# Two-layer hybrid decoder on one core: weights as the moving operand, 512 columns a matmul, in branches, projections and feed-forward

## Chip, cores and metric

One NeuronCore of a Trainium2 chip runs the whole program in one launch. The metric is the device time of an execution in microseconds (us); lower is better. Three runs of the kernel before were timed, and one execution was profiled.

## What is computed

The input x has 256 tokens of 1024 features, in float32. Two layers follow, then a last RMSNorm. Of a layer, cut to what matters here (three kinds of attention, a, b and c, stand between):

```python
def _hybrid_layer(x, ...):
    proj = _rms_norm(x, attn_norm) @ w_in          # 1024 -> 6816: q, k, v, latents, gates
    y_a = _diff_attention(...) @ w_branch_a        # 512 -> 1024
    y_b = _dilated_attention(...) @ w_branch_b     # 512 -> 1024
    y_c = _mla(...) @ w_branch_c                   # 512 -> 1024
    g_a, g_b, g_c = split(sigmoid(gates), 3)       # 3 x 1024 columns of proj
    x = x + (g_a * y_a + g_b * y_b + g_c * y_c) @ w_out
    h2 = _rms_norm(x, ffn_norm)
    return x + (silu(h2 @ w_ffn_gate) * (h2 @ w_ffn_up)) @ w_ffn_down    # 2816 hidden
```

## The kernel before

Every product is made in float32 precision from two parts: a weight or an activation is split into a high part `hi` (rounded to the fp32r type) and the rest `lo`, and a product is three fp32r matmuls, hi·hi, hi·lo and lo·hi (`mm3`, L160). A matmul has a stationary operand (128 x 128, loaded into the array) and a moving one that streams through it, 512 columns at most; in the profile `out<-moving,stationary` names them in this order.

**Weights.** `weight_plan` (L51) lists all weights in the order of use, in pieces of 128 partitions x 1024 numbers (512 KB). For each piece SP issues a DMA into one of 5 `raw` buffers, ScalarE (ACT) makes `whi` (`hi_of`, L171), VectorE (DVE) makes `wlo` (`lo_of`, L176), and TensorE (PE) uses both. `take` (L203) hands out the next piece and asks for a later one to be split.

**Activations** are kept with features on the partitions and the 256 tokens along the row (`xT`, four tiles of two feature blocks each). `pair_job` (L211) makes two blocks of 128 output features in one PSUM bank: for each of nk feature blocks, 2 x 3 matmuls, in which a 128 x 128 block of the weight is stationary and 256 tokens move:

```python
for c in range(2):
    s = slice(c * 128, c * 128 + 128)
    self.mm3(ps[:, c * 256:c * 256 + 256], wh[:, s], wl[:, s], xh[k], xl[k], ...)
```

It serves the q and k projections (`qk_proj`), the gates and branches (`branch`, L545), `w_out` and the layer-0 `w_ffn_down` (`out_proj`, L875) and gate and up (`ffn`, L889). The `v_proj` jobs (L463), `mla_up` and the latent inputs do it the other way round: 128 tokens of the activation are stationary and up to 512 weight columns move. So does `tail` (L932), the last layer's `w_ffn_down`.

**Norms.** The normed activation is split before its factor is known: `split_pair` multiplies by the gain alone, and the factor of each token (r) is applied when a result leaves PSUM, by a row `Rb` that is broadcast over the partitions. `norm_sums` (L340) adds squares over the partitions with four tiny matmuls against a tile of ones, `norm_rows` (L360) makes the row `Rb` with two matmuls. At the start GpSimd (POOL) makes the squares of x (L325, L329).

**Order.** The work is written as a stream of pieces (`dense`, `ffn`) from which `pump` takes steps between the stages of attention; a list scheduler then orders the instructions of each engine when the program is built. Near the end `token_major` (L921) transposes the residual on PE, 16 transposes in all, because `tail` produces token-major rows.

Of the kernel before, what the change touches and what calls it, by code (L numbers as in the profile page):

```python
# [34 lines left out]
N_FR = 24  # L35
N_KD = 5
# [14 lines left out]
def weight_plan():  # L51
# [11 lines left out]
    for l in range(DEPTH):  # L63
        block("w_in", l, KT, OFF_C, N_C)
        mixer_in(l, OFF_AQ)
        block("mla_w_uq", l, 3, 0, 768)
        block("mla_w_ukv", l, 2, 0, 1024)
        block("w_in", l, KT, OFF_AV, 512)
        mixer_in(l, OFF_BQ)
        block("w_in", l, KT, OFF_BV, 512)  # L70
        for br, name in BRANCHES:
            for p in range(4):
                block("w_in", l, KT, OFF_G + br * D + p * 256, 256)
                block(name, l, 4, p * 256, 256)
        for p in range(4):
            block("w_out", l, KT, p * 256, 256)
        for p in range(NF // 2):
            block("w_ffn_gate", l, KT, p * 256, 256)
            block("w_ffn_up", l, KT, p * 256, 256)
        if l + 1 < DEPTH:  # L80
            for p in range(4):
                block("w_ffn_down", l, NF, p * 256, 256)
        else:
            block("w_ffn_down", l, NF, 0, 1024)
# [41 lines left out]

def split_rows(t):
    return t.rearrange("p (c t) -> p c t", c=2)


class Build:
    def __init__(self, nc, tc, ctx, x, w, gains, lam, fnorm, cst, out):
        self.nc, self.tc = nc, tc
        self.x_in, self.w_in, self.gains_in = x, w, gains
# [9 lines left out]
        self.fr = ring(N_FR, 512, F32R, "fr")  # L144
        self.kd = ring(N_KD, 1024, F32R, "kd")
# [65 lines left out]
    def pair_job(self, ps, xh, xl, nk):  # L211
        k = 0
        while k < nk:
            for wh, wl in self.take():
                for c in range(2):
                    s = slice(c * 128, c * 128 + 128)
                    self.mm3(ps[:, c * 256:c * 256 + 256], wh[:, s], wl[:, s], xh[k], xl[k],
                             k == 0 and c == 0, k == nk - 1)
                k += 1
# [4 lines left out]
    def setup(self):  # L224
# [3 lines left out]
        self.xT = [cp.tile([128, 2, 256], F32, name=f"xT{p}") for p in range(4)]  # L228
        for p in range(4):
            if p == 0:  # L230
                nc.sync.dma_start(out=self.xT[0][:, 0], in_=self.x_in[:, 0, :])
                self.dma_piece()
                nc.sync.dma_start(out=self.xT[0][:, 1], in_=self.x_in[:, 1, :])
            else:
                nc.sync.dma_start(out=self.xT[p], in_=self.x_in[:, 2 * p:2 * p + 2, :])
# [70 lines left out]
    def split_pair(self, p, src, g0):  # L306
        hi, lo = self.fr.get(), self.fr.get()
        halves = [(slice(c * 256, c * 256 + 256), self.gains[:, g0 + 2 * p + c:g0 + 2 * p + c + 1]) for c in range(2)]
        for c, (cs, g) in enumerate(halves):
            self.hi_of(hi[:, cs], src[:, c], g)  # L310
        for c, (cs, g) in enumerate(halves):
            self.lo_of(lo[:, cs], src[:, c], hi[:, cs], g)
        self.xg += [hi, lo]
        self.xh += [hi[:, 0:256], hi[:, 256:512]]
        self.xl += [lo[:, 0:256], lo[:, 256:512]]

    def fresh_norm(self):
        self.xg, self.xh, self.xl = [], [], []

    def square_pair(self, p, first=False):  # L320
        nc = self.nc
        x = self.xT[p].rearrange("p c t -> p (c t)")
        if first:
            t = self.f.get()
            nc.gpsimd.tensor_tensor(out=t, in0=x, in1=x, op=ALU.mult)  # L325
            if p == 0:
                self.sq = t
            else:
                nc.gpsimd.tensor_tensor(out=self.sq, in0=self.sq, in1=t, op=ALU.add)  # L329
                self.f.put(t)  # L330
            return
        if p == 0:
            self.sq = self.f.get()
            nc.scalar.activation(out=self.sq, in_=x, func=AF.Square)
        else:
            t = self.f.get()
            nc.scalar.activation(out=t, in_=x, func=AF.Square)
            nc.vector.tensor_tensor(out=self.sq, in0=self.sq, in1=t, op=ALU.add)
            self.f.put(t)

    def norm_sums(self):
        nc = self.nc
        ps = self.att.get()
        nc.vector.tensor_tensor(out=self.sq[:, 0:256], in0=self.sq[:, 0:256], in1=self.sq[:, 256:512], op=ALU.add)
        for b in range(2):
            self.mm(ps[:, 2 * b:2 * b + 2], self.sq[:, b * 128:b * 128 + 128], self.ones[:, 0:2], b == 0, True)
        v = self.small()
        nc.vector.tensor_scalar(out=v, in0=ps[:, 0:4:2], scalar1=1.0 / D, scalar2=EPS, op0=ALU.mult, op1=ALU.add)  # L348
        self.att.put(ps)
        self.f.put(self.sq)  # L350
        self.r = self.cp.tile([128, 2], F32, name=f"r{self.n_norm}")
        self.n_norm += 1
        self.rsqrt(self.r, v)
        self.diag = self.fr.get()
# [16 lines left out]
    def first_norm(self, pump):  # L371
        self.fresh_norm()
        for p in range(4):
            self.split_pair(p, self.xT[p], G_ATT)
# [3 lines left out]
            self.square_pair(p, True)  # L378

# [1 line left out]
    def dense(self, l):  # L381
        self.pq = [self.banks.get() for _ in range(2)]
        self.pk = [self.att.get() for _ in range(2)]
        for k in range(KT):
            (wh, wl), = self.take()
            st, sp = k == 0, k == KT - 1
            for b in range(2):
                ts = slice(b * 128, b * 128 + 128)
                h, lo = self.xh[k][:, ts], self.xl[k][:, ts]
# [17 lines left out]
        self.m, self.mh, self.ml = [], [], []  # L407
# [4 lines left out]
    def key_pair(self, src, rows=slice(0, 128)):  # L412
        kd = self.kd.get()
        v = kd[rows].rearrange("p (c f t) -> p c f t", c=2, f=2)
        self.split(v[:, :, 0], v[:, :, 1], src)
# [41 lines left out]
    def v_proj(self, v, paired):  # L457
        pv = [self.banks.get() for _ in range(2)]
        k = 0
        while k < KT:  # L460
            for wh, wl in self.take():
                for b in range(2):
                    ts = slice(b * 128, b * 128 + 128)  # L463
                    self.mm(pv[b], self.xh[k][:, ts], wh, k == 0, False)
                    self.mm(pv[b], self.xh[k][:, ts], wl, False, False)
                    self.mm(pv[b], self.xl[k][:, ts], wh, False, k == KT - 1)
                k += 1
            if k < KT:
                yield
# [75 lines left out]
    def branch(self, o, first, last):  # L545
        nc = self.nc
        for p in range(4):
            bank = self.banks.get()
            yield from self.pair_job(bank, self.xh, self.xl, KT)
            t = self.f.get()  # L550
            nc.vector.tensor_tensor(out=split_rows(t), in0=split_rows(bank), in1=self.Rb, op=ALU.mult)  # L551
            self.banks.put(bank)
            nc.scalar.activation(out=t, in_=t, func=AF.Tanh, scale=0.5)
            yield
            yh = [a[:, c * 256:c * 256 + 256] for a in o[0] for c in range(2)]
            yl = [a[:, c * 256:c * 256 + 256] for a in o[1] for c in range(2)]
            bank = self.banks.get()
            yield from self.pair_job(bank, yh, yl, 4)
            if first:
                self.m.append(self.f.get())  # L560
                nc.vector.scalar_tensor_tensor(out=self.m[p], in0=t, scalar=1.0, in1=bank, op0=ALU.add, op1=ALU.mult)
            else:
                nc.vector.scalar_tensor_tensor(out=t, in0=t, scalar=1.0, in1=bank, op0=ALU.add, op1=ALU.mult)
                nc.vector.tensor_tensor(out=self.m[p], in0=self.m[p], in1=t, op=ALU.add)  # L564
            self.f.put(t)
            self.banks.put(bank)
            if last:
                hi, lo = self.fr.get(), self.fr.get()
                self.split(hi, lo, self.m[p], 0.5)
                self.f.put(self.m[p])  # L570
                self.mh.append(hi)
                self.ml.append(lo)
            yield
        self.fr.put(*o[0], *o[1])
# [146 lines left out]
    def out_tiles(self):  # L721
        return [self.fr.get() for _ in range(2)], [self.fr.get() for _ in range(2)]

    def unit_stages(self, kind, l, h):
# [4 lines left out]
        if kind == "a":  # L729
# [46 lines left out]
            def output():  # L776
# [5 lines left out]
                cs = slice((h % 2) * 256, (h % 2) * 256 + 256)  # L782
                self.split(self.oa[0][h // 2][:, cs], self.oa[1][h // 2][:, cs], pt[:, 0:256], self.gdiff[l])
# [5 lines left out]
        if kind == "b":  # L789
            def scores():  # L790
                k = self.kb[h // 2]
                u["s"] = self.scores(self.half(self.qb, h), k[:, (h % 2) * 512:(h % 2) * 512 + 512], self.tb[h])
                if h % 2 == 1:
                    self.fr.put(*self.qb[h // 2])
                    self.kd.put(k)

            def values():
# [10 lines left out]
                cs = slice((h % 2) * 256, (h % 2) * 256 + 256)  # L808
                self.split(self.ob[0][h // 2][:, cs], self.ob[1][h // 2][:, cs], po[:, 0:256])
# [10 lines left out]
        def scores():  # L820
# [3 lines left out]
            if c == 1:  # L824
                self.fr.put(*q)
                self.kd.put(k)

        def values():
# [16 lines left out]
            if c == 1:  # L845
                cs = slice((p % 2) * 256, (p % 2) * 256 + 256)
                self.split(self.oc[0][p // 2][:, cs], self.oc[1][p // 2][:, cs], t[:, 0:256])
# [228 lines left out]
```

## Time and profile before

| | |
|---|---|
| runs | 917.66, 914.79, 917.59 us; median 917.59 |
| profiled execution | span 916.3 us (the page gives no time beside its span) |
| PE busy | 904.6 us of it (99%), 6954 matmuls |
| DVE, ACT, POOL busy | 648.8 (71%), 503.6 (55%), 76.0 us (8%) |
| read from memory | 152.98 MB |

The span is the time from the first to the last instruction of the profiled execution; it lies 1.3 us under the median of the runs. A matmul's busy time runs from its start to the modelled end of its pipeline, and successive matmuls overlap, so what a matmul costs in a stream is read from start to start, and not from its mean duration.

### The profile page before, as it was taken

The page shows a single profiled execution, that of the slowest core. Times are in us where ns is not written, and L with a number is a line of the kernel's source. Part 1 is how long each engine was busy: PE and PEld are TensorE (multiplying, and loading weights), DVE is VectorE, ACT ScalarE, POOL GpSimd, SP SyncE. Part 2 cuts the span into 40 slices and gives each one's busy share as a digit, 9 for nine tenths or more (in the row PEclk, how much of TensorE's full clock was granted, in tenths as well). Part 3 has the DMA queues.
Part 4 walks back from the last instruction along what each step waited for, and adds up shares of the span by engine and source line. Part 5 has one row for each costly group of instructions (what it writes and reads, how often), then busy time and mean ns, then how long its engine had stood idle before and what let it go on. Part 6 is the DMA issues. An engine that isn't in the chain of part 4 may idle for free.

```text
span 916.3 us, 17319 instructions
## 1 busy us (share of the span) xinstructions
PE 904.6 (99%) x6954; PEld 877.5 (96%) x6954; DVE 648.8 (71%) x1069; ACT 503.6 (55%) x838; POOL 76.0 (8%) x98
## 2 busy tenths in 40 slices
PE   7999999999999999999999999999999999999997
PEld 6988999999999999999999899999999999999886
DVE  7777879866776777755457778896667776677544
ACT  5776768544554444444357867774445544544332
POOL 6730030000000000000011303100000000000000
PEclk8999999999999999999999999999999999999999
DMA  7754443455555555555575454345665665556641
GB/s 236 257 181 142 136 139 116 139 184 185 184 184 176 186 182 182 182 161 188 152 217 164 140 180 133 121 139 155 188 183 168 188 181 182 183 175 205 188 148 46
DMA packets 45440, 155.15 MB, mean 169 GB/s; under 512 B 5168, under 2 KB 6192, under 8 KB 45360
## 3 DMA queue, kind: packets, MB, share of 16 engines
q1 hardware_dynamic: 44928, 153.51, 53.8%
q8 instruction: 54, 0.88, 0.4%
q10 hardware_dynamic: 432, 0.55, 0.2%
q14 instruction: 26, 0.21, 0.1%
HBM read 152.98 MB, written 1.05 MB: 168 GB/s over the span
## 4 chain that ended last, share of the span: by engine, by line
PE 97%; DMA 1%; DVE 0%; issue 0%; ACT 0%; POOLq 0%; SPq 0%; DVEq 0%
PE bank L158 87%; PE att L158 7%; DMA raw<-w 1%; PE att L652 1%; PE att L701 0%; PE att L702 0%; PE att L703 0%; DVE fr L178 0%; PE att L626 0%; PE att L781 0%; PE att L926 0%; DVE wlo L176 0%; ACT whi L171 0%; ACT f L978 0%; POOLq L1071 0%
## 5 line engine op out<-in xcount | busy, mean ns | idle before, releaser
L158 PE MATMUL bank<-fr,whi 128*128 128x256 f32 x3520 | 642.1, 284 | 0.0
L158 PEld LDWEIGHTS bank<-fr,whi 128*128 128x128 f32 x3520 | 549.7, 192 | 0.2
L158 PE MATMUL bank<-fr,wlo 128*128 128x256 f32 x1760 | 499.6, 284 | 0.0
L171 ACT ACTIVATE whi<-raw 128x1024 fp32r<-128x1024 f32 (+3 forms) x296 | 305.9, 1035 | 349.0 <-PE bank L158 225.6
L176 DVE TENSOR_TENSOR wlo<-raw,whi 128x1024 fp32r<-128x1024 f32 (+3 forms) x296 | 355.3, 1203 | 164.5 <-ACT whi L171 163.7
L158 PEld LDWEIGHTS bank<-fr,wlo 128*128 128x128 f32 x1760 | 337.4, 192 | 0.0
L158 PE MATMUL bank<-whi,fr 128*128 128x512 f32 (+2 forms) x368 | 113.9, 377 | 0.4 <-ACT whi L171 0.3
L158 PEld LDWEIGHTS bank<-whi,fr 128*128 128x128 f32 x368 | 69.8, 193 | 10.4 <-ACT whi L171 0.9
L158 PE MATMUL bank<-wlo,fr 128*128 128x512 f32 (+2 forms) x184 | 67.5, 377 | 3.9 <-DVE wlo L176 3.9
L158 PEld LDWEIGHTS bank<-wlo,fr 128*128 128x128 f32 x184 | 35.3, 193 | 9.6 <-DVE wlo L176 5.1
L304 POOL TENSOR_TENSOR r<-small,mhalf 128x2 f32<-128x2 f32 x4 | 3.8, 939 | 488.7 <-DVE small L348 488.7
L171 ACT ACTIVATE fr<-f 64x512 fp32r<-64x512 f32 (+2 forms) x56 | 33.5, 598 | 13.0 <-DVE f L564 4.9
L693 ACT ACTIVATE s<-s,small 128x256 f32<-128x256 f32 x80 | 35.6, 450 | 2.1 <-DVE small L691 1.8
L304 POOL TENSOR_TENSOR small<-small,mhalf 128x2 f32<-128x2 f32 (+1 forms) x12 | 8.2, 684 | 293.0 <-DVE small L967 176.9
L158 PE MATMUL bank<-kd,whi 128*128 128x256 f32 x160 | 29.0, 283 | 0.0
L158 PE MATMUL att<-whi,fr 128*128 128x288 f32 (+1 forms) x88 | 25.7, 304 | 0.0
L176 DVE TENSOR_TENSOR fr<-f,fr 64x512 fp32r<-64x512 f32 (+2 forms) x40 | 25.2, 631 | 0.4
L158 PEld LDWEIGHTS bank<-kd,whi 128*128 128x128 f32 x160 | 25.0, 192 | 0.0
L551 DVE TENSOR_TENSOR f<-bank,row 128x512 f32<-128x512 f32 x24 | 16.5, 688 | 11.4 <-PE bank L158 11.4
L158 PE MATMUL bank<-whi,kd 128*128 128x512 f32 (+1 forms) x80 | 23.9, 364 | 0.0
L905 DVE SCALAR_TENSOR_TENSOR f<-bank,row 128x512 f32<-128x512 f32 x22 | 15.2, 690 | 11.4 <-PE bank L158 11.4
L897 DVE TENSOR_TENSOR f<-bank,row 128x512 f32<-128x512 f32 x22 | 15.2, 691 | 10.6 <-PE bank L158 10.5
(154 smaller groups left out, 825.5 us busy)
## 6 DMA issues: line engine op xcount, KB each, us to landing
raw<-w SPq DMA_DIRECT2D x270, 512.0 KB, 3.6
raw<-w SPq DMA_DIRECT2D x16, 336.0 KB, 3.1
raw<-w SPq DMA_DIRECT2D x6, 384.0 KB, 3.6
raw<-w SPq DMA_DIRECT2D x4, 256.0 KB, 2.6
xT<-x SPq DMA_DIRECT2D x3, 256.0 KB, 6.2
f<-fnorm SPq DMA_DIRECT2D x2, 256.0 KB, 3.6
out<-f ACTq DMA_DIRECT2D x2, 256.0 KB, 2.1
xT<-x SPq DMA_DIRECT2D x2, 128.0 KB, 3.1
```

The lines of the kernel that those rows point to most:

```text
L158: self.nc.tensor.matmul(out, lhsT, rhs, start=start, stop=stop, skip_group_check=True)
L171: self.nc.scalar.activation(out=hi, in_=src, func=AF.Copy, scale=scale)
L176: self.nc.vector.tensor_tensor(out=lo, in0=src, in1=h, op=ALU.subtract)
L304: self.nc.gpsimd.tensor_tensor(out=out, in0=v, in1=self.mhalf[:, 0:v.shape[1]], op=ALU.pow)
L551: nc.vector.tensor_tensor(out=split_rows(t), in0=split_rows(bank), in1=self.Rb, op=ALU.mult)
L652: nc.tensor.transpose(ps[0:96, c, b * 128:b * 128 + 128], src[:, b, 2 * p + c, :], self.ident)
L693: nc.scalar.activation(out=s[:, SL[b]], in_=s[:, SL[b]], func=AF.Exp, bias=mn[:, b:b + 1], scale=-1.0, accum_out=z[:, b:b + 1])
L897: nc.vector.tensor_tensor(out=split_rows(a), in0=split_rows(bank), in1=self.Rb, op=ALU.mult)
L905: nc.vector.scalar_tensor_tensor(out=split_rows(t), in0=split_rows(bank), scalar=0.5, in1=self.Rb, op0=ALU.mult, op1=ALU.mult)
```

## The change

In `branch`, `out_proj` and `ffn` the roles are exchanged. A new `rows_job` keeps 128 tokens of the activation stationary (hi, hi, lo) and moves 512 weight columns, into two banks, one for each half of the tokens. The weight plan has the same bytes in pieces of two feature blocks x 512 columns; gate and up alternate in one array `w_ffn`. `qk_proj` keeps `pair_job`. Results are now token-major, so that the norm's factor is a number per partition (`rh` = r/2 goes into the tanh as its scale, `rr` = r²/2 into the product), and the residual `x_tm` is kept token-major, from a second copy of x that is loaded at the start. What the next product needs feature-major is transposed on PE: the mixed branches (`mixed`), the residual before each norm but the first (`norm_pairs`) and the hidden activations (`hidden_pairs`). Squares are summed along the row by ACT (`squares`). `norm_sums`, `token_major` and POOL's squares go, and `norm_rows` stays for the two attention norms alone. The tiles `fr` and `kd` become one ring of 17 pairs. The core of the diff:

```diff
+    def rows_job(self, ps, x, nk):
+        k = 0
+        while k < nk:
+            for wh, wl in self.take():
+                for b in range(2):
+                    h, lo = (x[k][:, o + b * 128:o + b * 128 + 128] for o in (0, 256))
+                    self.mm(ps[b], h, wh, k == 0, False)
+                    self.mm(ps[b], h, wl, False, False)
+                    self.mm(ps[b], lo, wh, False, k == nk - 1)
+                k += 1
+            if k < nk:
+                yield
...
     def setup(self):
...
         for _ in range(N_RAW - 4):
             self.dma_piece()
+        for b in range(2):
+            nc.sync.dma_start(out=self.x_tm[b], in_=self.xt_in[b])
...
+    def squares(self, n):
+        for b in range(2):
             t = self.f.get()
-            nc.gpsimd.tensor_tensor(out=t, in0=x, in1=x, op=ALU.mult)
...
+            self.nc.scalar.activation(out=t, in_=self.x_tm[b][:, n * 512:n * 512 + 512], func=AF.Square, scale=D ** -0.5,
+                                      accum_out=self.ss[n][:, b:b + 1])
...
+    def transposed(self, src, c0):
+        bank = self.att.get()
+        ps = split_rows(bank)
+        for c in range(2):
+            for b in range(2):
+                self.nc.tensor.transpose(ps[:, c, b * 128:b * 128 + 128], src[b][:, c0 + c * 128:c0 + c * 128 + 128], self.ident)
+        return bank, ps
+
+    def norm_pairs(self, pairs, g0):
+        for p in pairs:
+            bank, ps = self.transposed(self.x_tm, p * 256)
+            self.split_pair(p, ps, g0)
+            self.att.put(bank)
...
     def branch(self, o, first, last):
-        for p in range(4):
-            bank = self.banks.get()
-            yield from self.pair_job(bank, self.xh, self.xl, KT)
-            t = self.f.get()
-            nc.vector.tensor_tensor(out=split_rows(t), in0=split_rows(bank), in1=self.Rb, op=ALU.mult)
...
+        for n in range(2):
+            bank = [self.banks.get() for _ in range(2)]
+            yield from self.rows_job(bank, self.xs, KT)
+            t = [self.f.get() for _ in range(2)]
+            for b in range(2):
+                nc.scalar.activation(out=t[b], in_=bank[b], func=AF.Tanh, scale=self.rh[:, b:b + 1])
...
+            yield from self.rows_job(bank, x, 4)
...
+    def mixed(self, n):
+        for p in range(2):
+            bank, ps = self.transposed(self.m[n], p * 256)
+            t = self.fr.pair()
+            self.split(*fields(t), ps, 0.5)
...
+    def out_proj(self, pairs, nk, g0, late):
...
+        for n in range(2):
+            bank = [self.banks.get() for _ in range(2)]
+            for i, _ in enumerate(self.rows_job(bank, ChunkList(pairs), nk)):
+                if n == 0 and i == 0:
+                    late()
+                if n == 1 and i == 1:
+                    self.norm_pairs((0, 1), g0)
...
+            for b in range(2):
+                x = self.x_tm[b][:, n * 512:n * 512 + 512]
+                self.nc.vector.tensor_tensor(out=x, in0=x, in1=bank[b], op=ALU.add)
...
+    def hidden_pairs(self, a, n):
+        for p in range(n // 256):
+            bank, ps = self.transposed(a, p * 256)
+            self.hp.append(self.fr.pair())
+            self.split(*fields(self.hp[-1]), ps)
...
     def ffn(self):
+        def gated(b, a, g):
+            nc.scalar.activation(out=a, in_=g, func=AF.Tanh, scale=self.rh[:, b:b + 1])
+            nc.vector.scalar_tensor_tensor(out=a, in0=a, scalar=1.0, in1=g, op0=ALU.add, op1=ALU.mult)
+        def product(b, a, u):
+            nc.vector.scalar_tensor_tensor(out=a, in0=a, scalar=self.rr[:, b:b + 1], in1=u, op0=ALU.mult, op1=ALU.mult)
+        for i in range(5):
+            a = [self.f.get() for _ in range(2)]
+            bank = [self.banks.get() for _ in range(2)]
+            for j, _ in enumerate(self.rows_job(bank, self.xs, KT)):
+                yield
+                if j == 1 and self.waiting:
+                    self.hidden_pairs(*self.waiting)
...
-    def token_major(self, b, f):
```

**Where rows moved.** Three places of the instruction lists. First PE inside a job of the feed-forward of layer 0. Before; the moving operand is an activation half (`fr`), the stationary one a 128-column block of a weight piece:

```order
L158 MATMUL bank1_62<-fr13_82,whi3_160 128x256
L158 MATMUL bank1_62<-fr9_78,wlo3_165 128x256
L158 MATMUL bank1_62<-fr15_84,whi4_161 128x256
L158 MATMUL bank1_62<-fr16_85,whi4_161 128x256
L158 MATMUL bank1_62<-fr15_84,wlo4_166 128x256
L158 MATMUL bank1_62<-fr15_84,whi4_161 128x256
L158 MATMUL bank1_62<-fr16_85,whi4_161 128x256
L158 MATMUL bank1_62<-fr15_84,wlo4_166 128x256
```

Now the same engine in the same feed-forward, in a gate job, where the hidden values of the step before (`f4`, `f7`, one for each half of the tokens) are turned over:

```order
L210 MATMUL bank0_61<-whi0_145,fr11_80 128x512
L443 MATMUL att1_66<-ident_188,f4_90 128x128
L443 MATMUL att1_66<-ident_188,f7_93 128x128
L443 MATMUL att1_66<-ident_188,f4_90 128x128
L443 MATMUL att1_66<-ident_188,f7_93 128x128
L443 MATMUL att3_68<-ident_188,f4_90 128x128
L443 MATMUL att3_68<-ident_188,f7_93 128x128
L443 MATMUL att3_68<-ident_188,f4_90 128x128
L443 MATMUL att3_68<-ident_188,f7_93 128x128
L210 MATMUL bank3_64<-whi1_146,fr13_82 128x512
L210 MATMUL bank3_64<-wlo1_151,fr13_82 128x512
L210 MATMUL bank3_64<-whi1_146,fr13_82 128x512
```

Matmuls are half as many and twice as wide, and eight transposes stand together between the second and the third of four pieces of a gate job.

Second, PE at the border from `w_out` to the feed-forward in layer 0, now. `bank2` is the last bank of `w_out`, `x_tm0` and `x_tm1` the residual of the two halves of the tokens, `fr15` the first pair of the normed activation:

```order
L443 MATMUL att3_68<-ident_188,x_tm1_158 128x128
L443 MATMUL att3_68<-ident_188,x_tm0_157 128x128
L443 MATMUL att3_68<-ident_188,x_tm1_158 128x128
L210 MATMUL bank2_63<-whi0_145,fr7_76 128x512
L443 MATMUL att2_67<-ident_188,x_tm0_157 128x128
L443 MATMUL att0_65<-ident_188,x_tm0_157 128x128
L210 MATMUL bank3_64<-whi1_146,fr15_84 128x512
L210 MATMUL bank3_64<-wlo1_151,fr15_84 128x512
L210 MATMUL bank0_61<-whi1_146,fr15_84 128x512
L210 MATMUL bank0_61<-wlo1_151,fr15_84 128x512
L443 MATMUL att2_67<-ident_188,x_tm1_158 128x128
```

All 16 transposes of this norm stand within 22 rows around the end of `w_out`, the first feed-forward matmuls among them; before, the four pairs were split as each pair of `w_out` was finished, without a transpose.

Third, ACT at the start, now, where the five first weight pieces are split and the sixth follows (`raw0` for the second time):

```order
L223 ACTIVATE whi3_148<-raw3_143 128x672
L223 ACTIVATE whi4_149<-raw4_144 128x672
L392 ACTIVATE f4_90,small1_107<-x_tm0_157 128x512
L392 ACTIVATE f6_92,small2_108<-x_tm0_157 128x512
L392 ACTIVATE f5_91,small1_107<-x_tm1_158 128x512
L392 ACTIVATE f7_93,small2_108<-x_tm1_158 128x512
L223 ACTIVATE whi0_145<-raw0_140 128x672
```

Before, the sixth piece was split right after the fifth; the four squares, which need the second copy of x, now stand ahead of it.

## Rows read from the trace of the kernel before

**Rows 1.** The page: span, PE's share, and the chain that ended last, by engine

```profile
span 916.3 us, 17319 instructions
...
PE 904.6 (99%) x6954; PEld 877.5 (96%) x6954; DVE 648.8 (71%) x1069; ACT 503.6 (55%) x838; POOL 76.0 (8%) x98
...
PE 97%; DMA 1%; DVE 0%; issue 0%; ACT 0%; POOLq 0%; SPq 0%; DVEq 0%
```

**Rows 2.** What PE waited for, whole span: total us, times, longest us

```profile
PE bank L158 <- DVE wlo L176: 3.9, 4, 2.1
PE bank L158 <- DVE ones L240: 1.0, 1, 1.0
PE bank L158 <- ACT whi L171: 0.3, 1, 0.3
```

**Rows 3.** The largest group of matmuls by form, PE: count, busy us, mean ns

```profile
L158 PE MATMUL bank<-fr,whi 128*128 128x256 f32 x3520 | 642.1, 284 | 0.0
```

**Rows 4.** The chain in order of time, layer 1's feed-forward: start us, us, what

```profile
743.41 0.44 PE att L926 x4
743.85 17.28 PE bank L158 x144
```

**Rows 5.** Timeline of PE in `v_proj` of layer 0, 512 columns: start us, us

```profile
76.91 0.39 PE L158 MATMUL bank<-wlo,fr 128*128 128x512 f32 x1
...
78.27 0.39 PE L158 MATMUL bank<-wlo,fr 128*128 128x512 f32 x1
```

**Rows 6.** Timeline of PE in `tail`, 512 columns

```profile
904.62 0.61 PE L158 MATMUL bank<-whi,fr 128*128 128x512 f32 x2
...
906.66 0.39 PE L158 MATMUL bank<-whi,fr 128*128 128x512 f32 x1
```

**Rows 7.** One tile's view, PE reads of xT: duration ns min/median/max

```profile
L926 PE MATMUL att<-ident,xT x16: 271/272/273, 743.2 to 796.7; 128*128 128x128 f32 x16
```

**Rows 8.** Timeline of PE around `norm_sums` of layer 0's feed-forward

```profile
280.25 0.51 PE L158 MATMUL att<-ones,f 128*128 128x2 f32 x4
...
280.82 0.40 PE L158 MATMUL bank<-fr,whi 128*128 128x256 f32 x2
```

**Rows 9.** By stretch: its us, busy us of PE, PEld, DVE, ACT, POOL; PEclk, DMA, GB/s

```profile
0.00:15.00 15.00, 10.63 (x53) 9.34 (x54) 10.16 (x14) 9.39 (x17) 8.17 (x11) 1.00 0.80 258
15.00:22.00 7.00, 6.00 (x22) 5.57 (x22) 6.88 (x8) 1.64 (x3) 5.32 (x6) 0.52 0.61 185
22.00:29.00 7.00, 7.00 (x48) 7.00 (x48) 3.61 (x13) 3.65 (x6) 4.94 (x5) 0.99 0.94 350
96.00:178.50 82.50, 82.50 (x666) 80.54 (x665) 73.08 (x194) 60.29 (x148) 10.28 (x12) 1.00 0.40 129
...
280.30:407.00 126.70, 126.70 (x1058) 126.70 (x1058) 89.33 (x105) 58.85 (x67) 0.71 (x1) 1.00 0.57 182
```

**Rows 10.** Timeline of PE at the start, weight pieces of the latent inputs

```profile
14.11 0.44 PE L158 MATMUL bank<-wlo,fr 128*128 128x384 f32 x1 [2.12 <-DVE wlo L176]
...
17.93 0.69 PE L158 MATMUL bank<-wlo,fr 128*128 128x384 f32 x1 [1.00 <-DVE wlo L176]
...
28.94 0.40 PE L158 MATMUL bank<-fr,whi 128*128 128x256 f32 x2
```

**Rows 11.** Timeline of DVE at the start

```profile
9.86 2.58 DVE L178 SCALAR_TENSOR_TENSOR fr<-xT,gains,fr 128x256 fp32r<-128x256 f32 x2
...
13.98 2.93 DVE L178 SCALAR_TENSOR_TENSOR fr<-xT,gains,fr 128x256 fp32r<-128x256 f32 x2
```

**Rows 12.** Timeline of ACT at the start: the sixth weight piece

```profile
13.64 0.76 ACT L171 ACTIVATE whi<-raw 128x672 fp32r<-128x672 f32 x1 [0.34 <-DMA raw<-w]
```

**Rows 13.** Groups by form, DVE: count, busy us, mean ns

```profile
L551 DVE TENSOR_TENSOR f<-bank,row 128x512 f32<-128x512 f32 x24 | 16.5, 688 | 11.4 <-PE bank L158 11.4
...
L178 DVE SCALAR_TENSOR_TENSOR fr<-att,gains,fr 128x256 fp32r<-128x256 f32 x10 | 4.4, 475 | 0.0
```

**Rows 14.** Groups by form, ACT

```profile
L337 ACT ACTIVATE f<-xT 128x512 f32<-128x512 f32 x9 | 5.5, 616 | 0.0
```

More of the change, by code (lines that the diff above doesn't have):

```diff
@@ L71, in weight_plan @@
         for br, name in BRANCHES:
-            for p in range(4):
[L73 to L79, printed above, removed]
+            for n in range(2):
+                block("w_in", l, KT, OFF_G + br * D + n * 512, 512)
+                block(name, l, 4, n * 512, 512)
+        for n in range(2):
+            block("w_out", l, KT, n * 512, 512)
+        for n in range(2 * FF // 512):
+            block("w_ffn", l, KT, n * 512, 512)
         if l + 1 < DEPTH:
-            for p in range(4):
-                block("w_ffn_down", l, NF, p * 256, 256)
+            for n in range(2):
+                block("w_ffn_down", l, NF, n * 512, 512)
         else:
@@ L124, in put, with __init__, get, pair @@
         self.free_tiles.extend(tiles)
+class PairRing:
+    def __init__(self, tiles):
+        self.whole = list(tiles)
+        self.halves = [(t[:, 0:512], t[:, 512:1024]) for t in tiles]
+        self.free = deque((i, h) for i in range(len(tiles)) for h in range(2))
+    def get(self):
+        free = set(self.free)
+        for lone in (True, False):
+            for i, h in self.free:
+                if not lone or (i, 1 - h) not in free:
+                    self.free.remove((i, h))
+                    return self.halves[i][h]
+        raise IndexError("no half is free")
+    def pair(self):
+        free = set(self.free)
+        for i, h in self.free:
+            if (i, 1 - h) in free:
+                self.free.remove((i, h))
+                self.free.remove((i, 1 - h))
+                return self.whole[i]
+        raise IndexError("no pair is free")
+    def put(self, *aps):
+        for a in aps:
+            for i, t in enumerate(self.whole):
+                if a is t:
+                    self.free.extend([(i, 0), (i, 1)])
+                for h in range(2):
+                    if a is self.halves[i][h]:
+                        self.free.append((i, h))
+def chunks(pairs):
+    return [t[:, c * 512:c * 512 + 512] for t in pairs for c in range(2)]
+class ChunkList:
+    def __init__(self, pairs):
+        self.pairs = pairs
+    def __getitem__(self, k):
+        return self.pairs[k // 2][:, (k % 2) * 512:(k % 2) * 512 + 512]
+def fields(t):
+    v = t.rearrange("p (c f t) -> p c f t", c=2, f=2)
+    return v[:, :, 0], v[:, :, 1]
 def split_rows(t):
@@ L341, in norm_sums @@
[L341 to L346, printed above, removed]
+        t = self.fr.pair()
+        hi, lo = fields(t)
+        gains = [self.gains[:, g0 + 2 * p + c:g0 + 2 * p + c + 1] for c in range(2)]
+        for c, g in enumerate(gains):
+            self.hi_of(hi[:, c], src[:, c], g)
@@ L436, in qk_proj @@
             bank = self.banks.get()
-            yield from self.pair_job(bank, self.xh, self.xl, KT)
+            yield from self.pair_job(bank, self.xs, KT)
             ps = split_rows(bank)
@@ L458, in v_proj @@
         pv = [self.banks.get() for _ in range(2)]
[L459 to L469, printed above, removed]
+        yield from self.rows_job(pv, self.xs, KT)
         for b in range(2):
@@ new lines, in ffn @@
+        a = [self.f.get() for _ in range(2)]
+        bank = [self.banks.get() for _ in range(2)]
+        for j, _ in enumerate(self.rows_job(bank, self.xs, KT)):
+            yield
+            if j == 1:
+                self.hidden_pairs(*self.waiting)
+        self.fr.put(*self.xg)
+        for b in range(2):
+            gated(b, a[b][:, 0:256], bank[b][:, 0:256])
+            product(b, a[b][:, 0:256], bank[b][:, 256:512])
+        self.banks.put(*bank)
+        self.waiting = (a, 256)
+        yield
@@ L933, in tail @@
+    def tail(self):
         nc = self.nc
@@ L1059 @@
     a = {k: np.asarray(v) for k, v in inputs.items()}
+    gate, up = a["w_ffn_gate"], a["w_ffn_up"]
+    a["w_ffn"] = np.concatenate([m[:, :, c:c + 512] for c in range(0, FF, 512) for m in (gate, up)], axis=2)
     w = pack_weights(a)
```

255 lines of the change are left out of this document (101 added, 154 removed).

## The prediction, made before the change was run

> **What bounds the kernel now.** I read the page first, and in it PE's share and the chain that ended last [rows 1]. PE is busy for 904.6 of 916.3 us, and 97% of the chain is PE. That alone doesn't prove that PE is the limit, since busy times of pipelined matmuls overlap. So I read what PE waited for next [rows 2]: the waits come to 5.2 us in the whole span, and they lie at the start. Between the start and the end the time is the number of matmuls times the distance from one start to the next; whoever wants it shorter has to change one of the two.
>
> That distance is what the change is about. The largest group by form [rows 3] says 284 ns for a matmul of 256 columns, but that is the duration, of which more than half overlaps with the next. In the chain 144 such matmuls take 17.28 us [rows 4]: **0.1200 us each**. For 512 columns the trace has the very form that the change spreads, activation still and weights moving: six starts in `v_proj` from 76.91 to 78.27 are 1.36 us [rows 5], and nine in `tail` from 904.62 to 906.66 are 2.04 us [rows 6]. Both give **0.2267 us**. At the full 2.4 GHz, 256 columns stream in 0.1067 us and 512 in 0.2133, so each matmul pays a fixed 13.3 ns whatever its width, and two matmuls of 256 joined in one save it once: 0.2400 - 0.2267 = 0.0133 us.
>
> Last I read who would be late if PE were faster [rows 9]. In the feed-forward stretch from 280.3 us DVE is busy for 89.3 of 126.7 us, ACT for 58.9, and the DMA engines for 57%. In attention, from 96 us, DVE is the nearest, 73.1 of 82.5 us.
>
> **The change, part by part.**
>
> *Matmuls.* `pair_job` issues 6 matmuls for each feature block and 256 output columns. The jobs that change have, in a layer, 12 x 48 + 12 x 24 = 864 in the branches, 4 x 48 = 192 in `w_out` and 22 x 48 = 1056 in gate and up; `w_ffn_down` of layer 0 has 4 x 132 = 528. That is 2 x 2112 + 528 = 4752 matmuls of 256 columns, which become 2376 of 512. The instruction lists agree (438 matmuls of 512 columns before, 2814 now). All of it is on the path: 2376 x 0.0133 = **-31.6 us**.
>
> *Transposes added.* 16 in each of the two `mixed` steps' layers (32), 16 for each of three norms (48), 44 for the hidden values of each layer (88): 168. In the stream four transposes take 0.44 us [rows 4]. 168 / 4 x 0.44 = **+18.5 us**, on PE and so on the path too.
>
> *PE work removed.* The 16 transposes of `token_major`, 4 x 0.44 = 1.8 us. `norm_sums`, four times: from 280.25 to 280.82 us stand its tiny matmuls and one of 256 columns [rows 8], so 0.57 - 0.12 = 0.45 us each, 1.8 us. `norm_rows` before the two feed-forwards, 4 x 0.12 = 0.5 us. Together **-4.1 us**.
>
> *Evictions and splits.* DVE no longer multiplies by `Rb`: for 512 gate and up columns it did ten passes of 512 numbers at 0.69 us [rows 13] and now does six, four from the banks and two for the splits of the transposed values. ACT has four squares at 0.62 us [rows 14] for each norm, as it had for all but the first, which POOL did. This is hidden work, cost nothing: PE's wait rows don't name it [rows 2]. Weight bytes are the same, and are to arrive 0.1200 x 2 / 0.2267 = 1.06 times as fast; 182 GB/s in the feed-forward stretch becomes 193, and the start has reached 258 and 350 [rows 9]. Cost nothing as well; if DVE's cover went in attention (73.1 of 82.5 us), what PE saves there, some 10 jobs' pieces, would be lost, under 2 us.
>
> *The new waits.* Every transposed value goes bank, DVE, PE, ACT and DVE, PE. In the rows of the feed-forward two of four pieces of a gate job lie before the transposes, 24 matmuls or 5.4 us, against two DVE passes of 0.69: covered, nothing. The narrow places are the three borders from `w_out` or `w_ffn_down` to what follows. There the last addition into `x_tm` (0.69 us) has only three wide matmuls and some transposes before the transposes that need it, and the first feed-forward matmul follows its split at a similar distance. Bounds: 0 where it just fits, and the addition and the first split in full where it doesn't, 0.69 + 0.48 [rows 13] = 1.2 us. I take 0.5 each, since the list shows nearly enough work ahead: **+1.5 us**.
>
> *The start.* Two things pull apart. POOL's squares go, and beside them DVE was slow: two splits of 256 took 2.58 and 2.93 us [rows 11], where one takes 0.475 undisturbed [rows 13]. That is 1.6 and 2.0 us too long on a chain for which PE waited 2.12 and 1.00 us [rows 10]; and from 15 to 22 us, after these waits, PE's granted clock was 0.52, its lower level of 1.2 GHz [rows 9], which costs about half of 7 us. On the other side the second copy of x, 1.05 MB, is queued ahead of the sixth weight piece, and ACT's four squares, which wait for it, stand ahead of that piece's split, which already waited for its DMA before [rows 12]. At 258 GB/s that is 4.1 us. Bounds: a gain of 3.1 for the two waits and 3.4 for the clock, were the weights in time; a loss of 4.1 for the bytes and another 3.4 for a second stretch at the low clock. In between PE has slack, as the latent inputs end at 28.94 us [rows 10] and their 96 matmuls, half of 384 columns and half of 288, need 48 x (0.160 + 0.120 + 2 x 0.0133) = 14.7 us at full clock. I take **-1.0 us**, near the middle, since each wait that goes is met by one that comes.
>
> *Sum:* -31.6 + 18.5 - 4.1 + 1.5 - 1.0 = -16.7 us. On the span, 916.3 becomes 899.6. The median of the runs is 1.3 above the profiled span, so the forecast is **900.9 us**.
>
> **The rivals.**
>
> *Transposes cost their duration (slower).* A transpose here loads a new stationary block for only 128 columns. Its duration is 272 ns [rows 7], its distance in the stream 0.11 us [rows 4], because four stand together and overlap. If the new ones, which read tiles just written and are in places strewn singly between wide matmuls, don't overlap, 152 more of them cost 152 x (0.272 - 0.11) = 24.6 us more: 925.5 us. It decides from 0.22 us per transpose on, where the saving of 16.7 is used up. Against it: the rows of four, and single ones in the list have a wide matmul of 0.2267 us beside them, under which a load can run. The Trainium skill ("TensorE: Matmul & The Clock Gate", Part 4: PE-mode transpose) gives about 275 ns for a transpose inside a kernel. By that rule the change would lose 152 x 0.165 = 25 us against my sum and be slower than before; the trace agrees with the figure as a duration, and denies it as a price. Chance 3%.
>
> *The fixed cost isn't per matmul.* If the 13.3 ns were not saved by joining, the matmuls would give nothing and the transposes remain: 916.3 + 18.5 - 4.1 + 1.5 - 1.0 + 1.3 = 932.5 us. Two places of the trace with 512 columns deny it, to a nanosecond [rows 5, 6]. The same page (Back-to-back issue gap) puts a fixed cost of about 2.5 ns on a matmul: by that the joining would be worth 5.9 us, and the change would be slower, 926.6 us; the measured 13.3 decides. Chance 1%.
>
> *Waits at every crossing.* There are 22 places where PE turns values over: ten in each layer, and two more for the norm of layer 1. If each exposed one DVE pass of 0.69 us, 15.2 us would go: 916.1, no change. For it: DVE also splits a weight piece of 1.2 us in between, which may stand in front. Against it: the 5.4 us of cover at 10 of the 22. Chance 4%.
>
> *Starved start.* Both losses at the start in full: 900.9 + 1.0 + 7.5 = 909.4 us. For it: the sixth piece already waited on its DMA [rows 12]. Chance 10%.
>
> *Fluent start.* Both gains: 900.9 + 1.0 - 6.5 = 895.4 us. Against it: the extra bytes. Chance 10%.
>
> **How the numbers follow.** The forecast has the remaining 72%. Its own spread is the borders (0 to 3.6 us), the transposes (0.10 to 0.12 us each, 1.7 us either way) and the start. The range reaches to the fluent start with cheap borders and transposes, 895.4 - 2 = **893**, and to the starved one, **909**. Left out are the first three rivals and the two ends' tails. Faster by over 0.3% of the median, which is about what a measurement of this kernel can tell from none, is below 914.8: forecast, both starts and part of the crossings, 0.93. Within it: the rest of the crossings, 0.03. Slower: 0.04.
>
> **What would show it.** Right: half as many matmuls of 512 columns in the branches, `w_out` and feed-forward, at 0.2267 us from start to start; four transposes in 0.44 us; a feed-forward stretch without PE waits; DVE's share down. Wrong: waits of PE for DVE or ACT after 30 us; a granted clock below 1.0 beyond the start; the first q and k matmul well after 28.9 us (starved) or before 26 (fluent); transposes that delay the next matmul by over 0.22 us each.

## The result, and the profile after

| | before | after |
|---|---|---|
| median of the runs | 917.62 us (914.79 to 918.12, 4 runs) | 895.41 us (894.39 to 896.65, 4 runs) |
| span of the profiled execution | 916.3 us | 894.8 us |

The ratio is 0.9775, with a 95% interval of 0.9752 to 0.9798: the change makes the kernel 2.2% faster, against 1.8% forecast. 895.41 us lies in the range of 893 to 909, 5.5 us below the forecast of 900.9.

Page of the changed kernel, to be held against [rows 1]: span, busy time by engine, chain that ended last.

```profile
span 894.8 us, 12732 instructions
...
PE 886.5 (99%) x4710; PEld 763.9 (85%) x4710; DVE 591.9 (66%) x990; ACT 504.5 (56%) x852; POOL 66.4 (7%) x91
...
PE 97%; DMA 1%; issue 1%; SPq 0%; ACT 0%; DVE 0%; POOLq 0%; POOL 0%
```

PE is the bound as before, with 97% of the chain. It has 2244 matmuls fewer, and they are wider, as the groups by form show (count, busy us, mean ns; against [rows 3]):

```profile
L210 PE MATMUL bank<-whi,fr 128*128 128x512 f32 x1876 | 592.4, 393 | 0.0
L210 PE MATMUL bank<-wlo,fr 128*128 128x512 f32 x938 | 366.4, 392 | 0.0
...
L443 PE MATMUL att<-ident,f 128*128 128x128 f32 x120 | 16.2, 272 | 0.0
...
L443 PE MATMUL att<-ident,x_tm 128*128 128x128 f32 x48 | 6.9, 272 | 0.0
```

1876 + 938 are the 2814 matmuls of 512 columns, 120 + 48 the 168 transposes. What they cost is read in the chain (start us, us, what), here in the feed-forward of layer 0, against [rows 4]:

```profile
290.49 0.87 PE att L443 x8
291.36 21.80 PE bank L210 x96
313.16 0.87 PE att L443 x8
```

Eight transposes take 0.87 us, 0.109 each, and 96 wide matmuls 21.80 us, 0.2271 each. No other engine stands between them. What PE waited for in the whole span (total us, times, longest), against [rows 2]:

```profile
PE bank L210 <- ACT whi L223: 1.1, 2, 0.9
PE bank L210 <- DVE ones L309: 1.0, 1, 1.0
```

These 2.1 us were 5.2, and none lies after 17 us: neither the borders nor the other crossings cost a wait. The stretches, against [rows 9] (columns as there):

```profile
0.00:15.00 15.00, 12.99 (x72) 12.07 (x73) 8.15 (x17) 10.45 (x20) 0.29 (x5) 1.00 0.86 303
15.00:22.00 7.00, 6.84 (x44) 6.29 (x43) 5.37 (x14) 5.44 (x10) 1.82 (x2) 1.00 1.05 399
22.00:29.00 7.00, 7.00 (x59) 7.00 (x58) 5.32 (x14) 6.84 (x18) 6.72 (x7) 1.00 0.88 332
...
280.30:407.00 126.70, 126.70 (x582) 105.24 (x582) 75.44 (x78) 58.42 (x66) 0.00 (x0) 1.00 0.63 191
```

In the feed-forward PE is busy without a gap, DVE has gone from 89.3 to 75.4 us of 126.7, and weights come at 191 GB/s, where 193 was worked out. The start is where the surprise lies: PE's clock stays at 1.00, POOL is nearly idle until 15 us, and the DMA engines bring 399 GB/s where they brought 185.

One sign that the prediction counts as wrong did come, a granted clock below 1.0 beyond the start: it is 0.66 from 55 to 60 us, with PE busy throughout. The kernel before has such a fall too, 0.80 and 0.86 from 60 to 65 and 65 to 70 us, so it is no difference between the two.

PE at the start, from the timeline; the last row is the first q and k matmul, as in [rows 10]:

```profile
8.52 0.44 PE L210 MATMUL bank<-whi,fr 128*128 128x384 f32 x1 [0.94 <-ACT whi L223]
...
16.57 0.44 PE L210 MATMUL bank<-whi,fr 128*128 128x384 f32 x1 [0.15 <-ACT whi L223]
...
22.72 0.40 PE L210 MATMUL bank<-fr,whi 128*128 128x256 f32 x2
```

And DVE's timeline, against [rows 11]:

```profile
9.27 0.88 DVE L230 SCALAR_TENSOR_TENSOR fr<-f,gains,fr 128x256 fp32r<-128x256 f32 x2
...
10.83 0.88 DVE L230 SCALAR_TENSOR_TENSOR fr<-f,gains,fr 128x256 fp32r<-128x256 f32 x2
```

Two splits take 0.88 us, where they took 2.58 and 2.93.

**Where the time went.** The first q and k matmul is the mark that divides the span: PE's work ahead of it is the same in both kernels, up to the norm's sums. It moved from 28.94 to 22.72 us, so 6.2 of the 21.5 us were won ahead of it and 15.3 behind it.

### The profile page after: what moved, and what is told of

It reads as the page before. It is cut to its first block, busy times and chain, and to the rows that moved or that the text cites. A ratio compares the mean times of both kernels' runs of the same rounds, so it can differ in the third digit from the quotient of the medians.

```text
span 894.8 us, 12732 instructions
## 1 busy us (share of the span) xinstructions
PE 886.5 (99%) x4710; PEld 763.9 (85%) x4710; DVE 591.9 (66%) x990; ACT 504.5 (56%) x852; POOL 66.4 (7%) x91
## 3 DMA queue, kind: packets, MB, share of 16 engines
HBM read 154.03 MB, written 1.05 MB: 173 GB/s over the span
## 4 chain that ended last, share of the span: by engine, by line
PE 97%; DMA 1%; issue 1%; SPq 0%; ACT 0%; DVE 0%; POOLq 0%; POOL 0%
PE bank L210 85%; PE att L210 7%; PE att L443 2%; DMA x_tm<-xt 1%; PE att L718 1%; PE att L767 0%; PE att L769 0%; PE att L768 0%; ACT f L392 0%; SPq L242 0%; PE att L692 0%; PE att L851 0%; DVE x_tm L1043 0%; SPq L302 0%; ACT x_tm L1058 0%
## 5 line engine op out<-in xcount | busy, mean ns | idle before, releaser
L210 PE MATMUL bank<-whi,fr 128*128 128x512 f32 (+1 forms) x2032 | 632.6, 387 | 1.1 <-ACT whi L223 1.1
L228 DVE TENSOR_TENSOR wlo<-raw,whi 128x1024 fp32r<-128x1024 f32 (+2 forms) x294 | 353.3, 1203 | 250.3 <-ACT whi L223 249.1
L223 ACT ACTIVATE whi<-raw 128x1024 fp32r<-128x1024 f32 (+2 forms) x294 | 305.0, 1040 | 309.8 <-PE bank L210 255.3
L210 PEld LDWEIGHTS bank<-whi,fr 128*128 128x128 f32 x2032 | 380.4, 188 | 73.9 <-ACT whi L223 1.6
L210 PE MATMUL bank<-wlo,fr 128*128 128x512 f32 (+1 forms) x1016 | 390.6, 386 | 0.0
L210 PEld LDWEIGHTS bank<-wlo,fr 128*128 128x128 f32 x1016 | 191.3, 188 | 36.3 <-DVE wlo L228 0.9
L210 PE MATMUL bank<-fr,whi 128*128 128x256 f32 x512 | 95.3, 285 | 0.0
L210 PEld LDWEIGHTS bank<-fr,whi 128*128 128x128 f32 x512 | 80.1, 191 | 0.2
L210 PE MATMUL bank<-fr,wlo 128*128 128x256 f32 x256 | 73.0, 285 | 0.0
L210 PEld LDWEIGHTS bank<-fr,wlo 128*128 128x128 f32 x256 | 49.0, 191 | 0.0
L614 ACT ACTIVATE f<-bank,rh 128x512 f32<-128x512 f32 x24 | 16.3, 689 | 8.7 <-PE bank L210 8.5
```

The costliest lines, as they stand in the source:

```text
L210: self.nc.tensor.matmul(out, lhsT, rhs, start=start, stop=stop, skip_group_check=True)
L223: self.nc.scalar.activation(out=hi, in_=src, func=AF.Copy, scale=scale)
L228: self.nc.vector.tensor_tensor(out=lo, in0=src, in1=h, op=ALU.subtract)
L614: nc.scalar.activation(out=t[b], in_=bank[b], func=AF.Tanh, scale=self.rh[:, b:b + 1])
```

## The experiments

The theory is the sum of the prediction with the fluent start in place of its own. The rivals are that another amount per matmul was won and another lost per transpose, so that two errors hide each other; and that the start owes its gain to something else than POOL. Beside the experiments the kernel before ran again, with medians of 915.25, 916.11 and 916.44 us (13, 19 and 13 runs).

**e1_halves: the wide matmuls cut in two.** All else, transposes and layouts too, stays as in the changed kernel.

```diff
-                    self.mm(ps[b], h, wh, k == 0, False)
-                    self.mm(ps[b], h, wl, False, False)
-                    self.mm(ps[b], lo, wh, False, k == nk - 1)
+                    w = 256 if halves else 512
+                    for c in range(512 // w):
+                        s = slice(c * w, c * w + w)
+                        self.mm(ps[b][:, s], h, wh[:, s], k == 0 and c == 0, False)
+                        self.mm(ps[b][:, s], h, wl[:, s], False, False)
+                        self.mm(ps[b][:, s], lo, wh[:, s], False, k == nk - 1)
```

> The changed kernel with each 512-column matmul of the exchanged jobs issued as two of 256 columns, activation still held, weights still moving; v_proj keeps 512. Same products and order, 2376 matmuls more. If the gain of the joining is a fixed 13.3 ns per matmul: +31.6 us, 895.4 becomes about 927, so slower than the kernel before by some 1%. If the gain came from elsewhere (the evictions without the broadcast row, the order, the start): within 3 us of 895.

Measured: 927.27 us (926.9 to 927.38, 4 runs), 31.9 us above the changed kernel, and 1.0116 of the kernel before (1.0099 to 1.0133). The chain of its feed-forward:

```profile
299.09 0.87 PE att L446 x8
299.97 23.03 PE bank L210 x192
```

192 matmuls of 256 columns in 23.03 us are 0.1199 each; the same columns in 96 matmuls took 21.80. So the joining is worth about what the sum said, and without it the change would be a loss: the transposes would be paid for nothing.

**e2_twice: every new transpose issued twice**, into the same place.

```diff
-            for b in range(2):
+            for b in (0, 0, 1, 1):
```

> The changed kernel with each of the 168 added transposes issued twice into the same place. If a transpose costs its distance in a stream, 0.11 us, as four in 0.44 us: +18.5 us, about 914. If it costs its duration, 0.272 us: +45.7 us, about 941. If transposes run in holes of the stream: no change, 895.

Measured: 914.31 us (912.72 to 914.83, 10 runs), 18.9 us above the changed kernel for 168 more transposes: 0.1125 us each. Its chain:

```profile
291.78 1.75 PE att L443 x16
293.52 21.81 PE bank L210 x96
```

16 stand in 1.75 us, 0.109 each, and the wide matmuls behind them are not slower; 168 x 0.109 = 18.3 us. The price per transpose is the distance in the stream and not the duration.

**e3_pool_squares: POOL's squares put back** into the changed kernel's start. Their result is not used; only the work is there.

```diff
+            t = self.f.get()
+            self.nc.gpsimd.tensor_tensor(out=t, in0=self.x0[p], in1=self.x0[p], op=ALU.mult)
+            if p == 0:
+                sq = t
+            else:
+                self.nc.gpsimd.tensor_tensor(out=sq, in0=sq, in1=t, op=ALU.add)
+                self.f.put(t)
+        self.f.put(sq)
```

> The changed kernel with POOL's four squares and three sums of x at the start put back, their result unused. If their load on POOL made DVE slow at the start and so cost PE waits and the low clock: the first q and k matmul comes 3 to 7 us later than 22.7 us, the granted clock falls below 1.0 between 10 and 25 us, and the time rises to 898 to 902. If the start became shorter for another reason (the token-major norm, the order of the rows): 895, first q and k matmul at 22.7.

Measured: 899.74 us (898.78 to 900.57, 4 runs), 4.3 us above the changed kernel. DVE's timeline shows the splits of [rows 11] slow again:

```profile
10.60 2.70 DVE L230 SCALAR_TENSOR_TENSOR fr<-f,gains,fr 128x256 fp32r<-128x256 f32 x2
...
15.05 1.91 DVE L230 SCALAR_TENSOR_TENSOR fr<-f,gains,fr 128x256 fp32r<-128x256 f32 x2
```

PE's timeline shows the same wait for a weight's low part back, and the mark at 26.72 us, 4.0 later:

```profile
15.19 0.45 PE L210 MATMUL bank<-wlo,fr 128*128 128x384 f32 x1 [2.35 <-DVE wlo L228]
...
26.72 0.40 PE L210 MATMUL bank<-fr,whi 128*128 128x256 f32 x2
```

PE's waits for DVE's low parts come to 3.7 us, where it had none. ACT's squares waited twice for a buffer that POOL held, 0.5 us each, which is a side effect of this experiment. The clock did not fall: in the profiled execution it stayed at 1.00 from 10 to 25 us, against that part of the expectation, so a low clock at the start is no part of the 4.3 us. The profiled span is 897.2 us, only 2.4 above the changed kernel's, because this execution lacks the fall of the clock behind the start (897.2 - 26.72 = 870.5 us behind the mark, against 872.1).

**e5_before_act_squares: the same from the other side**, in the kernel before. The squares of x are made by ACT and added by DVE.

```diff
-            self.square_pair(p, True)
+            self.square_pair(p)
```

> The kernel before with one part of the change alone: the squares of x at the start are made by ACT and added by DVE, not by POOL; the rest as before. If POOL's squares slowed DVE and so the start: the first q and k matmul comes 3 to 6 us before 28.9 us and the time falls to 912 to 915 (ratio about 0.995). If they did not: 917.6, or slower by the 2 us of additions that DVE now has at the start.

Measured: 913.5 us (912.39 to 915.55, 10 runs), 0.9977 of the kernel before (0.9965 to 0.9988), 2.6 us. Part of the 2.6 can be the clock: 6 of those 19 runs of the kernel before, and none of these 10, had a mean granted clock under 0.994. Two splits take 0.87 us, although DVE has the additions on top, PE waits for no low part, and the mark lies at 23.35 us (28.94 in [rows 10], 27.10 in e7 below). Not all of that reaches the end, as PE's timeline shows behind the mark:

```profile
23.35 0.40 PE L158 MATMUL bank<-fr,whi 128*128 128x256 f32 x2
...
26.92 0.33 PE L626 MATMUL att<-ident,f 128*128 128x128 f32 x1 [0.55 <-ACT f L585]
...
29.27 0.39 PE L158 MATMUL att<-fr,ones_r 128*128 128x256 f32 x1 [0.58 <-DVE fr L178]
```

Two waits, 1.1 us together, come next, which the changed kernel doesn't have.

**e4_xt_late: the second copy of x behind the sixth weight piece**, its squares behind that piece's split.

```diff
-        for b in range(2):
-            nc.sync.dma_start(out=self.x_tm[b], in_=self.xt_in[b])
...
+            if p == 2:
+                for b in range(2):
+                    self.nc.sync.dma_start(out=self.x_tm[b], in_=self.xt_in[b])
```

> The changed kernel with the second copy of x loaded after the sixth weight piece and ACT's four squares behind that piece's split. If the 1.05 MB and the squares ahead of the sixth piece still cost PE time: 0.5 to 4 us faster than 895.4. If the start has slack for them: 895, or a little slower, as the norm's factor comes later.

Measured: 895.56 us (894.01 to 895.74, 4 runs) against 895.41: the medians show no difference. The profiled executions do: the mark comes 0.9 us earlier, at 21.84, and the span is 893.8, 1.0 less. ACT's timeline has the split of the sixth weight piece at 12.47 us:

```profile
12.47 0.77 ACT L223 ACTIVATE whi<-raw 128x672 fp32r<-128x672 f32 x1 [0.31 <-DMA raw<-w]
```

The changed kernel has it at 15.77, two pieces in a row:

```profile
15.77 1.47 ACT L223 ACTIVATE whi<-raw 128x672 fp32r<-128x672 f32 x2
```

So the copy and its squares do make that piece 3.3 us later. But PE, with the five pieces before it to work through, gets to it only at about 16.3 us and waits 0.15. The chain of the changed kernel runs through the copy at this place:

```profile
5.54 7.63 DMA x_tm<-xt
```

PE thus has slack for most of the delay, and not for all of it: the copy costs about 0.9 us by one profiled execution of each kernel, which the medians of four runs each don't confirm.

**e6_before_more_bytes: the bytes alone**, as a load of 1.05 MB into four free buffers in the kernel before, behind the fifth weight piece. Nothing reads it.

```diff
+        dead = [self.f.get() for _ in range(4)]
+        for i, t in enumerate(dead):
+            nc.sync.dma_start(out=t, in_=self.xt_in[i // 2][:, (i % 2) * 512:(i % 2) * 512 + 512])
+        self.f.put(*dead)
```

> The kernel before with 1.05 MB more loaded at the start behind the fifth weight piece, where the change loads its second copy of x; nobody reads it. If the DMA queue is full there, as the forecast assumed with 258 GB/s: +2 to +4 us, 920 to 922. If it has room: 917.6, the sixth weight piece landing less than 1 us later than at 13.6 us.

Measured: 916.52 us (914.94 to 918.93, 10 runs), 1.0007 of the kernel before (0.9994 to 1.002): the time shows no cost. The other part of the expectation failed. The sixth weight piece was to land less than 1 us later, and ACT gets to split it at 16.32 us, 2.7 us later than in [rows 12]:

```profile
16.32 2.46 ACT L171 ACTIVATE whi<-raw 128x672 fp32r<-128x672 f32 x3 [3.00 <-DMA raw<-w]
```

Its stretches:

```profile
0.00:15.00 15.00, 11.46 (x55) 10.18 (x56) 10.06 (x14) 8.71 (x15) 7.95 (x12) 1.00 0.88 291
15.00:22.00 7.00, 5.33 (x35) 4.77 (x33) 4.34 (x7) 2.94 (x4) 1.94 (x2) 1.00 0.80 272
```

291 and 272 GB/s stand where the kernel before had 258 and 185: over these 22 us the DMA engines had room for the bytes, although the piece behind them came later. The delay hardly reaches PE, which waits for DVE here: the mark lies at 27.42 us. PE's clock is 1.00 from 15 to 22 us, although POOL works and PE waits 3.7 us for DVE. That made the 0.52 of [rows 9] doubtful as a property of the kernel, and so both kernels were profiled once more.

**e7_before_again and e8_after_again: both kernels unchanged.**

> The kernel before once more, to see which part of its start is the same in a second execution. If the low granted clock (0.52 from 15 to 22 us) belongs to the kernel, the clock is low again and the first q/k matmul starts at 28.9 us. If it belonged to that one execution, the clock is 1.00 throughout, the first q/k matmul starts at 27 to 27.5 us as in the run with more bytes, and the span is about 914.5 us. The waits for the weights' low parts stay in both cases (3 to 4 us in total). The time equals the kernel before.

> The changed kernel once more. The start is expected to repeat if POOL's work was what slowed it: first q/k matmul at 22 to 23 us, granted clock 1.00, waits of PE of 2 us in total, span 894 to 896 us. If the first profile was a lucky one, the mark lies at 24 us or later.

Measured: 915.06 us (914.36 to 916.22, 10 runs), 0.9985 of the kernel before's other runs (0.9973 to 0.9997), and 895.76 us (894.71 to 896.79, 4 runs). The start of the kernel before in this second execution, stretches:

```profile
0.00:15.00 15.00, 10.79 (x53) 9.67 (x54) 10.42 (x14) 9.51 (x17) 8.33 (x11) 1.00 0.80 258
15.00:22.00 7.00, 5.29 (x35) 5.01 (x34) 6.92 (x8) 1.55 (x3) 5.35 (x6) 1.00 0.59 176
```

and PE's timeline:

```profile
14.14 0.44 PE L158 MATMUL bank<-wlo,fr 128*128 128x384 f32 x1 [2.12 <-DVE wlo L176]
...
17.96 0.44 PE L158 MATMUL bank<-wlo,fr 128*128 128x384 f32 x1 [1.71 <-DVE wlo L176]
...
27.10 0.40 PE L158 MATMUL bank<-fr,whi 128*128 128x256 f32 x2
```

The waits are there again, the second 0.7 us longer, and PE's waits for low parts come to 4.9 us, more than the 3 to 4 expected; the low clock is not. The mark comes 1.8 us earlier (0.3 earlier than in e6), and the span is 914.4. The changed kernel has its mark at 22.92 us and a span of 895.0. So the waits belong to the kernel and the low clock to the execution. From e7 to the changed kernel the mark moves by 4.4 us and the rest by 15.2 (914.4 - 27.10 = 887.3 against 894.8 - 22.72 = 872.1). Each of these two executions has one fall of the clock behind the mark, to 0.66 in a stretch of 5 us (60 to 65 and 55 to 60 us), so the 15.2 compares like with like.

## Why the prediction was right, and where a term was off

The direction and the range were right. The median lies 5.5 us below the forecast: 4.8 of them come from the start (-6.2 us, where -1.0 and the 0.45 of the first `norm_sums` stood), 0.7 from the distance of median and span (0.6 after, 1.3 assumed), and nothing from the rest (-15.3, where -15.2 stood). The 0.7 is no property of the kernels: each run that is listed with its span is 1.7 to 1.9 us longer than it, so the distance only tells where the profiled execution lies among the runs.

What came is the rival of the fluent start, to which the prediction gave 10%, with its sign, the mark before 26 us. That its 895.4 us were met so closely is luck: of its two gains the waits gave more than the 3.1 us set, the clock gave less than its 3.4, and what the clock gave belongs to one execution.

- **Joining the matmuls, -31.6 us: right.** e1 takes it back and costs 31.9 us by the medians and 925.4 - 894.8 = 30.6 by the profiled spans. The profile has 0.1199 and 0.2271 us a matmul. The fixed cost per matmul is 2 x 0.1199 - 0.2271 = 12.7 ns by these rows, and 31.9 / 2376 = 13.4 ns by the runs. The Trainium skill ("TensorE: Matmul & The Clock Gate", Back-to-back issue gap) has about 2.5 ns, for the gap of a single matmul and not for a stream with weight loads; by it e1 would have cost an estimated 2376 x 2.5 ns = 5.9 us. For this kernel's fp32r matmuls the measurement decides. The rival that joining saves nothing falls.
- **Transposes, +18.5 us: right.** e2 gives 18.9 us for as many. The rival that they cost their duration would have had e2 at 168 x 0.272 = 46 us. The 275 ns of the Trainium skill (same page, Part 4: PE-mode transpose) agree with the 272 ns of a row's duration and are not what one costs between others.
- **PE work removed, borders and crossings, -4.1 + 1.5 + 0 us: right in sum.** The borders show no wait, so the +1.5 was not spent there. That the rest of the span comes out as forecast all the same needs 1.5 us from elsewhere, and where is not shown. Up to 1.0 may be the joining, by the 30.6 above and by the feed-forward's 0.2271 us a matmul for 0.2267; but 89 wide matmuls without a transpose among them, from 269.70 to 289.87 us, start 0.2266 us apart.
- **Evictions, splits, weight traffic, 0: right.** DVE's share fell, and PE waits for nobody in the feed-forward.
- **The start, -1.0 us: the term that was mis-sized. It measured -6.2, the 0.45 of the first `norm_sums` included.** The two gains were named rightly: the waits, and the clock. The failed step is the balance, "each wait that goes is met by one that comes". The wait that was to come is PE's for the sixth weight piece, behind the second copy of x, and the 4.1 us for it were wrong twice. First, a later piece is not a waiting PE: the piece is 3.3 us later through the copy and its squares (e4), and PE waits 0.15 us for it and is about 0.9 later in all by the profile of e4. The slack of PE, which the prediction itself names, covers the rest. Second, 258 GB/s was taken as the ceiling of the DMA engines. It is the mean over a stretch that begins with 2 us at 16 GB/s and in which the queue waits 1.5 us for a free weight buffer. A narrow stretch of the kernel before, 10 to 12 us, shows 402:

```profile
10.00:12.00 2.00, 1.99 (x12) 1.72 (x12) 2.00 (x2) 2.00 (x5) 2.00 (x2) 1.00 1.05 402
```

At 402 GB/s the 1.05 MB take 2.6 us, and 2.7 is what e6 shows as the delay of the sixth piece; there, too, it doesn't become a wait, since DVE is later still. Of the 6.2 us, 4.0 are POOL's squares (e3), 0.4 fit the first `norm_sums`, which together make up the 4.4 between e7 and the changed kernel, and 1.8 are the low clock that the first profile happened to have (e7). The clock had been priced at 3.4 us, half of 7. Of the difference 0.7 is that PE at full clock reaches its next wait earlier and waits 0.7 us longer there (e7), and 0.5 that PE waited for 1.0 of the 7 us; the remaining 0.4 is not placed.

The clock's part is no gain of the change. Against e7, an execution of the kernel before whose start ran at full clock, 914.4 us, the change is worth 19.6 us: 4.4 at the start and 15.2 behind it. The run times of the kernel before spread over some 4 us, and the clock goes with them: of its 55 runs beside the experiments and in e7, the 14 with a mean granted clock of 0.992 or 0.993 took 917.5 to 918.5 us, the 41 with 0.994 or more 914.1 to 917.2. Where in those runs the clock fell is not known, as they have no profile.

## What to carry to other kernels

When matmuls stand back to back, their number counts beside their columns: read the distance from start to start at two widths, and the difference per column pays, or doesn't, for the transposes that wider matmuls need. Price those transposes by their distance in a stream too. And don't take a transfer rate averaged over a stretch as a ceiling: look for the fastest narrow stretch first, and ask whether the queue was waiting for buffers. Then ask when the engine needs what comes later: a piece that is 3.3 us late made PE wait 0.15 us here.

## What the runs showed of the hardware

- **POOL's element-wise work slows DVE.** A split of 256 columns, which reads two operands from SBUF, takes 0.44 us with POOL idle (0.88 for two) and up to 1.47 with POOL at work (2.93 for two). POOL's own squares take 1.04 us at best and 1.37 beside DVE's splits. The Trainium skill ("SBUF — State Buffer", Who interferes with whom) says that a DVE instruction with two SBUF inputs contends with a GpSimd instruction that reads SBUF, and that the port pair they share is locked by one at a time. The lengthening of 1.0 us a split is about one POOL instruction of 1.04 us, which agrees: 0.44 + 1.04 = 1.48.
- **The same waits didn't always cost the clock.** With PE waits of 2.12 and 1.00 us the granted clock was 0.52 from 15 to 22 us, its lower level of 1.2 GHz for most of it; with waits of 2.12 and 1.71 (e7), 2.35 (e3) or 1.90 and 1.51 us (e6) it stayed at 1.00. Nor does a fall need a wait: in the changed kernel the clock was 0.50 from 56 to 59 us, and PE had waited for nothing since 17 us. One profile is not enough to book such a stretch as a cost of the kernel.
